# Differential attention and latent attention: row tiles turned by transposing transfers in place of TensorE transposes

## The chip, the cores and the metric

One core of a Trainium2 chip runs the kernel. The metric is the device time of one launch in microseconds (us). The kernel before takes 2170.72 us, the median of three runs (2170.44 to 2171.89).

## The reference

A decoder trunk of two layers over 256 tokens of 2048 values, all in 32-bit floats. Layer 0 has differential attention (8 heads, each with two query and two key parts of 128, of which the first 32 values are rotated by position), layer 1 multi-head latent attention (16 heads; each query has 128 plain and 64 rotated values). Behind each stands cross-attention into 256 memory tokens and a squared-ReLU MLP, and each of these adds its result to the residual stream. Cut to what the change touches:

```python
q = partial_rope(q.reshape(B, S, 2 * DA_HEADS, DA_HEAD_DIM), cos, sin, DA_ROT)
k = partial_rope(k.reshape(B, S, 2 * DA_HEADS, DA_HEAD_DIM), cos, sin, DA_ROT)
...
s = jnp.einsum('bqhcd,bkhcd->bhcqk', qi, k).astype(jnp.float32) * scale
p = jax.nn.softmax(s, axis=-1)
a = (p[:, :, 0] - lam * p[:, :, 1]).astype(v.dtype)
o = jnp.einsum('bhqk,bkhd->bqhd', a, v)
o = rms_norm(o, subln) * (1.0 - lambda_init)
return o.reshape(B, S, D_MODEL) @ wo
...
q = (c_q @ wuq).reshape(B, S, MLA_HEADS, MLA_NOPE + MLA_ROPE)
q = jnp.concatenate([q[..., :MLA_NOPE], apply_rope(q[..., MLA_NOPE:], cos, sin)], axis=-1)
```

## The kernel before

**Matrix products.** Every 32-bit product is made of three passes on TensorE, high by high, high by low, low by high. A job is 1 MB of weights: `load` (L189) fetches it on SP's queue into one of seven `raw` buffers, ScalarE casts each half to its high part (`whi`, L221) and VectorE subtracts for the low part (`wlo`, L222), four buffers each. A half serves 12 matmuls 512 wide for each of two row tiles of 128 tokens.

**Layer 0** goes through its heads in four groups, 0 to 3 (`attention`). For each group `project_diff` makes a chunk of 512 queries, of keys and of values; `heads_T` takes a finished row tile out of the accumulator with its scale (ScalarE), rotates it (`rope`, six operations on POOL), and turns it, so that heads stand on the partitions; then it is split into high and low parts (`split`, L366 on ScalarE and L367 on VectorE). Scores, softmax and weighted values of a group (`attend_diff`) run as side tasks between the chunks of the next. `normed` norms the weighted values of a row tile and turns them for the output product. The output weights are multiplied in pairs, by seven products of sums in place of eight; for some of the sums a second load is added onto a `raw` buffer by an accumulating load that POOL issues (L1003). In group 3 those pair products (`pr`) alternate with the projections (here: the weave).

**Turning a tile** goes in two ways. On TensorE: four transposes of 128x128 (`flip`, L174, called by `transpose4`) into a bank of the accumulator, or into a further one (`side_bank`, with `spare`). By transfers: ScalarE copies the tile as two planes of 16-bit words (`half_words`, L377), POOL issues a 256 KB store of them to a buffer in DRAM (`turned`, L379), SP issues a transposing transfer back (`turned_by_dma`, L384, tile `landed`). The second way is taken for group 1's queries and keys, group 2's queries, the weighted values of groups 0 and 1, and parts of the MLP.

**Layer 1** holds the rotated queries of two groups at a time in one buffer (`rotary_queries`, L1708 to L1733): two pieces of four heads each; a piece is rotated on POOL, written with its high part (L1721, ScalarE) and its low part (L1722, VectorE) side by side, and turned on TensorE through a side bank.

**What sets the order.** TensorE executes in the order in which the program issues. Side tasks are generators: one yields the time that its next step needs at least (`T_ROT` 12, `T_SHORT` 11, `T_LAND` 7, `T_TURN` 2.6 us by the program's own clock), and `pump` takes whichever is due between matmuls. The order on ScalarE, VectorE and POOL is set by a scheduler when the kernel is built; loads on SP, transposing transfers and accumulating loads stay in program order. Each engine executes its own list in order, and a wait at its head holds what is behind.

Of the kernel before, what the change touches and what calls it, by code (L numbers as in the profile page):

```python
# [18 lines left out]
P = 128  # L19
D = 2048  # L20
S = 256
NT = 2
# [30 lines left out]
def trunk(ctx, tc, x, xT, xT0, mem, memT, positions, gcols, gfinal, lam_vecs, consts, W, out):  # L53
    nc = tc.nc
# [77 lines left out]
    class Held:  # L132


        def __init__(self, tile=None):
            self.held = tile
            self.tasks = []
            self.part = None

        @property  # L140
# [21 lines left out]
    def give_back():  # L162
        free_banks[0] += 1
# [403 lines left out]

    def heads_T(ps, t, scale, dst, rot=None, spare=False, given=None, by_dma=False):


        def task():
            while given and not given():
                yield 0.5
            e = evacuate(ps, scale() if given else scale)
            if rot:
                cos, sin, heads, half = rot
                rope(e.rearrange("p (h d) -> p h d", h=heads), cos, sin, heads, half)
            if by_dma:
                yield T_ROT - 3.0 if rot else 0.2
                there = half_words(e)  # L580
                yield T_SHORT
                landed = turned_by_dma(there)
                yield T_LAND
                split(dst, t, landed)
                yield T_TURN
                return
            yield T_ROT + (14.0 if given else 0.0) if rot else T_EV
            b = ps
            if spare:
                b = yield from side_bank()  # L590
            split(dst, t, transpose4(e, b))
            if spare:
                give_back()
            yield T_TURN

        dst.run(task())
# [152 lines left out]
    def attend_diff(q, k, v, dst, coef, subcols, slack=0.0):  # L749
# [34 lines left out]
        def normed(t, blocks, out):  # L784
# [11 lines left out]
            )  # L796
            if dst.part:
                yield T_NORM
                give_back()
                there = half_words(os)  # L800
                yield T_SHORT
                landed = turned_by_dma(there)
                yield T_LAND
                split(dst, t, scaled(landed, subcols, dst.part(t)))
                yield T_TURN
                return
# [415 lines left out]
    ahead = raw_tile()  # L1222
# [173 lines left out]
    def attention(project, attend, mid, gcol, pairs=()):  # L1396
# [6 lines left out]
        for gi in range(4):  # L1403
            o = Held()
            if pairs and gi < 2:
                o.part = lambda t, gi=gi: pairs["A"].part(t, gi)
                first.append(o)
            attend(held, o)
            if pairs and gi == 2:
# [165 lines left out]
    def project_diff(gi):  # L1575
        q, k = Held(), Held()
        for i, dst in enumerate((q, k)):
            ps = matmul_chunk(acts, by_k=gi == i == 0)
            for t in range(NT):
                heads_T(  # L1580
                    ps[t], t, (lambda i=i, t=t: da_scales[i][t]) if gi == 0 else da_scales[i][t], dst, (cos[:, t, :hd], sin[:, t, :hd], 4, hd),
                    spare=gi == 3, given=(lambda: da_scales) if gi == 0 else None, by_dma=gi == 1 or (gi, i) == (2, 0),
                )
# [119 lines left out]
    def rotary_queries(gi):  # L1703
# [5 lines left out]

        def rotated(i, qr, ahead):  # L1710

            for task in ahead:
                yield task
            for t in range(NT):
                rope(rows[t][:, i], cos[:, t, hd:], sin[:, t, hd:], 4, hm)
            yield T_ROT
            es = []
            for t in range(NT):
# [3 lines left out]
                nc.vector.tensor_tensor(e[:, :, 64:], o, e[:, :, 0:64], ALU.subtract)  # L1722
                es.append(e)
            yield T_EV
            for t in range(NT):
# [8 lines left out]
        for i in range(2):  # L1734
            qr = Held(both[:, 4 * i : 4 * i + 4])
            qr.run(rotated(i, qr, ahead))
            ahead = qr.tasks
            rotary[gi + i] = qr
# [168 lines left out]
```

## Time and profile before

| | |
|---|---|
| time, median of 3 runs | 2170.72 us |
| the profiled execution's span | 2169.0 us |
| TensorE busy | 2155.4 us (99%) |
| VectorE busy | 1740.2 us (80%) |
| ScalarE busy | 1465.6 us (68%) |
| POOL busy | 221.0 us (10%) |
| moved by DMA | 543.89 MB, mean 251 GB/s |
| transposing transfers | 66 |

PE is TensorE's matmuls, PEld its weight loads, DVE VectorE, ACT ScalarE, POOL GpSimd, SP SyncE; SPq is SP's DMA queue. In a row of the timeline stand the start and the length in us, engine, line, operation, output and inputs by the program's names, the shape and a count; in brackets the idle time ahead of it and what ended that.

### The profile page before, as it was taken

Reading aid. Unit: us, or ns where it says so; the run is one execution under the profiler, and the core shown is the slowest. Engines: PE = TensorE matmul, PEld = TensorE weight load, DVE = VectorE, ACT = ScalarE, POOL = GpSimd, SP = SyncE. Lnnn points to the kernel's source line nnn. Section 1 sums busy time; section 2 is a strip of 40 time slices with the busy share of each in tenths; the row PEclk is TensorE's granted clock in tenths of the full one; section 3 lists DMA queues with packets and bytes.
Section 4 is the critical chain, followed back from the end, with each engine's and each line's share of the span. In section 5 each row is a group of like instructions: output and inputs, shape, how many; then the busy total and the mean of one; then the engine's idle time right before and its main releaser. Section 6 shows DMA issues by size and latency. Waiting matters only on the chain.

```text
span 2169.0 us, 27519 instructions
## 1 busy us (share of the span) xinstructions
PE 2155.4 (99%) x10187; PEld 1805.5 (83%) x10187; DVE 1740.2 (80%) x1962; ACT 1465.6 (68%) x1938; POOL 221.0 (10%) x336
## 2 busy tenths in 40 slices
PE   9999999999999999999999999999999999999998
PEld 7888888888888888888889988888888888888887
DVE  6656878788788889788886878778888888888887
ACT  7556756666767777776665755666777778677665
POOL 1113210001000000000000420000000000000001
PEclk9999999999999999999999999999999999999999
DMA  9477896548989999998986344645998999999895
GB/s 386 151 248 234 260 293 222 194 151 267 297 280 267 308 282 256 319 274 260 306 251 218 103 170 155 221 168 182 283 299 292 258 317 280 266 285 310 254 315 149
DMA packets 151863, 543.89 MB, mean 251 GB/s; under 512 B 79536, under 2 KB 79920, under 8 KB 92848
## 3 DMA queue, kind: packets, MB, share of 16 engines
q1 hardware_dynamic: 134496, 440.14, 56.9%
q0 software_dynamic: 16800, 101.20, 22.5%
q8 instruction: 80, 1.31, 0.2%
q10 hardware_dynamic: 432, 0.79, 0.1%
q14 instruction: 55, 0.45, 0.1%
HBM read 505.38 MB, written 19.40 MB: 242 GB/s over the span
## 4 chain that ended last, share of the span: by engine, by line
PE 95%; DVE 3%; DMA 1%; issue 1%; ACT 0%; DVEq 0%; POOLq 0%; POOL 0%
PE mm L170 62%; PE pr L170 28%; PE ax L170 3%; DVE wlo L222 1%; DMA raw<-in_mlp_wup_dram 1%; PE ax L174 1%; PE mm L174 1%; DVE raw L887 0%; DVE unit L391 0%; ACT whi L221 0%; DVE x L545 0%; DMA raw<-in_da_wqkv_dram 0%; PE pr L174 0%; DVE p L680 0%; DVE ev L1722 0%
## 5 line engine op out<-in xcount | busy, mean ns | idle before, releaser
L222 DVE TENSOR_TENSOR wlo<-raw,whi 128x1024 fp32r<-128x1024 f32 (+3 forms) x946 | 1138.8, 1217 | 335.5 <-ACT whi L221 313.7
L221 ACT CAST whi<-raw 128x1024 fp32r<-128x1024 f32 (+2 forms) x945 | 985.3, 1045 | 576.8 <-PE mm L170 420.0
L170 PE MATMUL mm<-whi,unit 128*128 128x512 f32 (+2 forms) x4000 | 1271.2, 389 | 1.3 <-DVE unit L391 0.9
L170 PEld LDWEIGHTS mm<-whi,unit 128*128 128x128 f32 x4000 | 749.1, 188 | 149.6 <-DVE unit L391 1.7
L170 PE MATMUL mm<-wlo,unit 128*128 128x512 f32 (+2 forms) x2000 | 774.1, 387 | 0.2
L170 PE MATMUL pr<-whi,unit 128*128 128x512 f32 x1912 | 610.5, 389 | 0.0
L170 PEld LDWEIGHTS mm<-wlo,unit 128*128 128x128 f32 x2000 | 376.2, 188 | 72.8 <-DVE wlo L222 3.0
L170 PEld LDWEIGHTS pr<-whi,unit 128*128 128x128 f32 x1912 | 358.8, 188 | 73.4
L170 PE MATMUL pr<-wlo,unit 128*128 128x512 f32 x956 | 372.3, 389 | 1.5 <-DVE wlo L222 1.5
L170 PEld LDWEIGHTS pr<-wlo,unit 128*128 128x128 f32 x956 | 179.7, 188 | 40.0 <-DVE wlo L222 3.6
L379 POOL DMA_DIRECT2D turned<-planes x66 | 37.7, 572 | 673.5 <-ACT planes L377 661.2
L887 DVE TENSOR_TENSOR raw<-raw,raw 128x2048 f32<-128x2048 f32 x40 | 91.5, 2288 | 8.8 <-DMA raw<-in_mlp_wup_dram 8.6
L545 DVE TENSOR_TENSOR x<-x,mm 128x512 f32<-128x512 f32 x128 | 85.3, 682 | 14.1 <-PE mm L170 14.0
L879 POOL DMA_DIRECT2D raw<-in_mlp_wup_dram x48 | 43.4, 905 | 447.8 <-DVE wlo L222 445.2
L431 POOL TENSOR_TENSOR rs<-rs,mhalf 128x1 f32<-128x1 f32 (+1 forms) x26 | 24.9, 962 | 408.1 <-DVE rs L430 408.0
L222 DVE TENSOR_TENSOR wlo<-unit,whi 128x1024 fp32r<-128x1024 f32 x48 | 57.3, 1221 | 5.2 <-ACT whi L221 4.0
L221 ACT CAST whi<-unit 128x1024 fp32r<-128x1024 f32 x48 | 49.8, 1053 | 9.7 <-PE pr L170 9.7
L377 ACT COPY planes<-p 128x1024 uint16<-128x1024 uint16 x48 | 50.0, 1041 | 0.3
L170 PE MATMUL mm<-unit,whi 128*128 128x256 f32 x256 | 46.9, 285 | 0.0
L425 ACT ACTIVATE junk<-x 128x512 bf16<-128x512 f32 (+1 forms) x57 | 35.3, 620 | 10.1 <-DVE x L1092 5.0
L1457 ACT ACTIVATE p<-p,r 128x512 f32<-128x512 f32 x42 | 30.4, 724 | 16.4 <-DVE p L962 7.4
L170 PEld LDWEIGHTS mm<-unit,whi 128*128 128x128 f32 x256 | 40.2, 192 | 0.3
(199 smaller groups left out, 1280.7 us busy)
## 6 DMA issues: line engine op xcount, KB each, us to landing
raw<-in_mlp_wdown_dram SPq DMA_DIRECT2D x128, 1024.0 KB, 7.3
raw<-in_mlp_wup_dram SPq DMA_DIRECT2D x120, 1024.0 KB, 6.9
raw<-in_mlp_wup_dram POOLq DMA_DIRECT2D x48, 1024.0 KB, 9.1
raw<-in_da_wqkv_dram SPq DMA_DIRECT2D x45, 1024.0 KB, 9.8
turned<-planes POOLq DMA_DIRECT2D x66, 256.0 KB, 6.4
raw<-in_da_wo_dram SPq DMA_DIRECT2D x16, 1024.0 KB, 7.0
raw<-in_ca_wkv_dram SPq DMA_DIRECT2D x16, 1024.0 KB, 6.7
raw<-in_mlp_wdown_dram POOLq DMA_DIRECT2D x16, 1024.0 KB, 10.7
```

Of the source, the lines that this page charges most:

```text
L170: return nc.tensor.matmul(o, stationary, moving, start=start, stop=stop, skip_group_check=onto)
L174: nc.tensor.transpose(o, src, ident)
L221: nc.scalar.copy(hi, r)
L222: nc.vector.tensor_tensor(lo, r, f32(hi), ALU.subtract)
L377: nc.scalar.copy(planes, src.bitcast(U16).rearrange("p (w s) -> p s w", s=2))
L379: nc.gpsimd.dma_start(there.rearrange("(q s) w -> q s w", s=2), planes)
L425: return nc.scalar.activation(junk[:, : src.shape[1]], src, AF.Square, scale=scale, accum_out=acc)
L431: nc.gpsimd.tensor_tensor(r[:, :n], r[:, :n], mhalf.broadcast_to([P, n]), ALU.pow)
L545: nc.vector.tensor_tensor(xc, xc, ps, ALU.add)
L879: tc.keep_in_program_order(nc.gpsimd.dma_start(onto, src, accum_op=ALU.add))
L887: nc.vector.tensor_tensor(o, o, q, ALU.add)
L1457: nc.scalar.activation(r, src, AF.Relu, scale=rstd[t])
```

## The change

Eighteen row tiles leave the first way for the second: the queries and keys of groups 0 and 3 and the keys of group 2 (ten tiles), the weighted values of group 2 (two, by the new mark `sent`), and in layer 1 three of the four held pieces of rotated queries (six tiles; the first piece stays on TensorE). TensorE has 72 transposes fewer; ScalarE has 18 copies to planes, POOL 18 stores and SP 18 transposing transfers more. For group 0 the step ahead of the turn waits `T_ROT + 14`. In `rotary_queries` the rotation is a task of its own, and a piece's rotation waits for that of the piece before, no longer for its transposes. The branch with a spare bank goes.

```diff
-    def heads_T(ps, t, scale, dst, rot=None, spare=False, given=None, by_dma=False):
+    def heads_T(ps, t, scale, dst, rot=None, given=None, by_dma=False):
...
             if by_dma:
-                yield T_ROT - 3.0 if rot else 0.2
+                yield T_ROT + (14.0 if given else -3.0) if rot else 0.2
                 there = half_words(e)
                 yield T_SHORT
                 landed = turned_by_dma(there)
@@
-            yield T_ROT + (14.0 if given else 0.0) if rot else T_EV
-            b = ps
-            if spare:
-                b = yield from side_bank()
-            split(dst, t, transpose4(e, b))
-            if spare:
-                give_back()
+            yield T_EV
+            split(dst, t, transpose4(e, ps))
@@
-            if dst.part:
+            if dst.part or dst.sent:
...
-                split(dst, t, scaled(landed, subcols, dst.part(t)))
+                split(dst, t, scaled(landed, subcols, dst.part and dst.part(t)))
@@
+            o.sent = bool(pairs) and gi == 2
@@
-                    spare=gi == 3, given=(lambda: da_scales) if gi == 0 else None, by_dma=gi == 1 or (gi, i) == (2, 0),
+                    given=(lambda: da_scales) if gi == 0 else None, by_dma=True,
@@
-        def rotated(i, qr, ahead):
-
+        def turned_rows(i, ahead):
             for task in ahead:
                 yield task
             for t in range(NT):
                 rope(rows[t][:, i], cos[:, t, hd:], sin[:, t, hd:], 4, hm)
             yield T_ROT
+
+        def rotated(i, qr, roped):
+
+            yield roped
...
+            if gi + i:
+                sent = [half_words(e.rearrange("p h d -> p (h d)")) for e in es]
+                yield T_SHORT + T_EV
+                es = [turned_by_dma(there) for there in sent]
+                yield T_LAND
+                for t in range(NT):
+                    nc.scalar.copy(qr[:, :, t * P : (t + 1) * P], es[t])
+                yield T_TURN
+                return
@@
             qr = Held(both[:, 4 * i : 4 * i + 4])
-            qr.run(rotated(i, qr, ahead))
-            ahead = qr.tasks
+            ahead = [Task(turned_rows(i, ahead))]
+            qr.run(rotated(i, qr, ahead[0]))
```

The order moves at three places. VectorE, start of the weave, before. `wlo` are splits of weights, `rs_2112` is the row norm on which POOL's first accumulating load (into `raw_1940`) waits:

```order
212 L1092 TENSOR_TENSOR x_84<-x_84,pr_2212 128x512
213 L437 TENSOR_REDUCE tot_2110<-ss_2093 128x1
214 L760 TENSOR_TENSOR rsum_2160<-rsum_2160,coef 128x4
215 L222 TENSOR_TENSOR wlo_2030<-raw_2027,whi_2029 128x1024
216 L430 TENSOR_SCALAR rs_2112<-tot_2110 128x1
217 L766 TENSOR_SCALAR a_2163<-p_2154,rsum_2160 128x128 x2
218 L654 TENSOR_TENSOR ax_2250<-ax_2250,mask 128x2x128
219 L222 TENSOR_TENSOR wlo_2034<-raw_2027,whi_2033 128x1024
220 L767 SCALAR_TENSOR_TENSOR a_2163<-p_2154,rsum_2160,a_2163 128x128
221 L624 RECIPROCAL rsum_2203<-ssum_2198 128x2
222 L767 SCALAR_TENSOR_TENSOR a_2163<-p_2154,rsum_2160,a_2163 128x128
```

And now; the norm is `rs_2119`, the accumulated buffer `raw_1948`:

```order
207 L223 TENSOR_TENSOR wlo_2033<-raw_2030,whi_2032 128x1024
208 L223 TENSOR_TENSOR wlo_2037<-raw_2030,whi_2036 128x1024
209 L1347 COPY memr_2098<-rs_2095 128x1
210 L650 TENSOR_TENSOR ax_2221<-ax_2221,mask 128x512
211 L223 TENSOR_TENSOR wlo_2132<-raw_2129,whi_2131 128x1024
212 L611 TENSOR_REDUCE nmax_2235<-ax_2221 128x4
213 L438 TENSOR_REDUCE tot_2117<-ss_2100 128x1
214 L431 TENSOR_SCALAR rs_2119<-tot_2117 128x1
215 L223 TENSOR_TENSOR wlo_2136<-raw_2129,whi_2135 128x1024
216 L1347 COPY memr_2122<-rs_2119 128x1
```

The norm stood behind the first half of an output product's weights (`raw_2027`). It now stands behind both halves of those (`raw_2030`) and the first half of the projection's weights after them (`raw_2129`).

POOL, in the weave, before: group 3's queries are rotated (`ev_2511`), then come accumulating loads; nothing is stored:

```order
110 L564 TENSOR_TENSOR rope_2516<-ev_2511,sin 128x4x16
111 L565 TENSOR_TENSOR ev_2511<-rope_2513,rope_2514 128x4x16
112 L566 TENSOR_TENSOR ev_2511<-rope_2515,rope_2516 128x4x16
113 L1003 DMA raw_1940<-in_da_wo_dram 128x2048
114 L1003 DMA raw_2417<-in_da_wo_dram 128x2048 x2
115 L561 TENSOR_TENSOR rope_2824<-ev_2822,cos 128x4x16
```

POOL at the same place now. `turned_2542` and `turned_2643` are group 2's weighted values, `turned_2590` and `turned_2594` group 3's queries:

```order
114 L380 DMA turned_2542<-planes_2540 128x1024
115 L564 TENSOR_TENSOR rope_2490<-ev_2486,cos 128x4x16
116 L565 TENSOR_TENSOR rope_2491<-ev_2486,sin 128x4x16
117 L566 TENSOR_TENSOR ev_2486<-rope_2488,rope_2489 128x4x16
118 L567 TENSOR_TENSOR ev_2486<-rope_2490,rope_2491 128x4x16
119 L999 DMA raw_1948<-in_da_wo_dram 128x2048
120 L999 DMA raw_2395<-in_da_wo_dram 128x2048
121 L432 TENSOR_TENSOR rs_2561<-rs_2561,mhalf 128x2
122 L380 DMA turned_2590<-planes_2588 128x1024
123 L380 DMA turned_2594<-planes_2592 128x1024
124 L380 DMA turned_2643<-planes_2641 128x1024
125 L999 DMA raw_2395<-in_da_wo_dram 128x2048
```

The stores of group 3's queries stand behind two accumulating loads.

SP, the same stretch, before: weight loads alone:

```order
86 L189 DMA raw_2567<-in_da_wo_dram 128x2048
87 L189 DMA raw_2591<-in_da_wqkv_dram 128x2048
88 L189 DMA raw_2661<-in_da_wqkv_dram 128x2048
89 L189 DMA raw_2707<-in_da_wqkv_dram 128x2048
90 L189 DMA raw_2742<-in_da_wo_dram 128x2048
91 L189 DMA raw_2766<-in_da_wqkv_dram 128x2048
```

SP now:

```order
93 L190 DMA raw_2598<-in_da_wqkv_dram 128x2048
94 L385 DMA_TRANSPOSE landed_2651<-turned_2542 128x4x256
95 L190 DMA raw_2659<-in_da_wqkv_dram 128x2048
96 L385 DMA_TRANSPOSE landed_2698<-turned_2590 128x4x256
97 L385 DMA_TRANSPOSE landed_2700<-turned_2594 128x4x256
98 L190 DMA raw_2709<-in_da_wqkv_dram 128x2048
99 L385 DMA_TRANSPOSE landed_2742<-turned_2643 128x4x256
100 L190 DMA raw_2751<-in_da_wo_dram 128x2048
101 L190 DMA raw_2780<-in_da_wqkv_dram 128x2048
102 L190 DMA raw_2867<-in_da_wqkv_dram 128x2048
```

Four transposing transfers stand between the loads; a load behind one of them is issued after it.

More of the change, by code (lines that the diff above doesn't have):

```diff
@@ L138, in __init__ @@
             self.part = None
+            self.sent = False
         @property
```

## The prediction

> **What bounds the kernel now.** I read the page first, the head for the span, the busy times and the shares of the chain that ended last.
>
> ```profile
> span 2169.0 us, 27519 instructions
> PE 2155.4 (99%) x10187; PEld 1805.5 (83%) x10187; DVE 1740.2 (80%) x1962; ACT 1465.6 (68%) x1938; POOL 221.0 (10%) x336
> PE 95%; DVE 3%; DMA 1%; issue 1%; ACT 0%; DVEq 0%; POOLq 0%; POOL 0%
> ```
>
> TensorE is the bound nearly everywhere: 95% of the chain. What it does not execute is time won one for one, as long as its inputs come as early as before; the question is what they come through then. The span is 1.7 us under the median of the runs (2170.7). I make the sum as a difference to the span and put the same difference to the median. About 0.2%, 4.3 us, is what a measurement of this kernel can tell from no change, so the median has to come under 2166.4 to count as faster and over 2175.1 to count as slower.
>
> Next the costs of the two routes: TensorE's own rows around one batch of eight transposes, then each step of the route by transfer (ns min/median/max, and us to landing).
>
> ```profile
> 62.00 0.39 PE L170 MATMUL mm<-whi,unit 128*128 128x512 f32 x1
> 62.23 1.03 PE L174 MATMUL mm<-identr,ev 128*128 128x128 f32 x8
> 63.02 0.48 PE L170 MATMUL mm<-whi,unit 128*128 128x512 f32 x1
> 63.34 0.40 PE L170 MATMUL mm<-wlo,unit 128*128 128x512 f32 x1
> 63.57 0.62 PE L170 MATMUL mm<-whi,unit 128*128 128x512 f32 x2
> ...
> L377 ACT COPY planes<-ev x14: 1032/1042/1053, 103.3 to 1531.2; 128x1024 uint16<-128x1024 uint16 x14
> ...
> L379 POOL DMA_DIRECT2D turned<-planes x66: 539/572/760, 104.7 to 1995.0; - x66
> ...
> DMA to landing us min/median/max: 2.3/6.4/9.0
> ...
> L384 SPq DMA_TRANSPOSE landed<-turned x66: 1227/1634/9474, 115.1 to 2014.3; - x66
> ...
> DMA to landing us min/median/max: 3.1/6.0/14.0
> ```
>
> Matmuls overlap, so the price of one is the distance of starts, not its length. A 512-wide one costs 63.57 - 63.34 = 0.23 us. From 62.23 to 63.34 lie eight transposes and one such matmul: 1.11 - 0.23 = 0.88, so 0.11 us a transpose.
>
> Third, how busy the stages are into which the new transfers fall. Columns: sum, PE, PEld, DVE, ACT, POOL, granted clock, share of the 16 DMA engines, GB/s.
>
> ```profile
> 60.00:80.00 20.00, 20.00 (x98) 16.74 (x97) 11.91 (x13) 10.56 (x13) 0.00 (x0) 1.00 0.40 149
> 80.00:100.00 20.00, 20.00 (x104) 16.89 (x102) 14.38 (x28) 12.35 (x27) 1.73 (x6) 1.00 0.16 52
> 220.00:230.00 10.00, 10.00 (x51) 8.45 (x50) 9.87 (x23) 9.74 (x28) 2.41 (x2) 1.00 0.60 240
> 240.00:320.00 80.00, 80.00 (x377) 66.87 (x376) 62.07 (x67) 49.11 (x60) 20.47 (x33) 1.00 0.98 302
> 1180.00:1300.00 120.00, 119.27 (x785) 109.37 (x784) 95.12 (x151) 76.24 (x139) 36.29 (x64) 1.00 0.43 152
> ```
>
> Group 0 (60 to 100 us) and the latent layer (1180 to 1300) have DMA engines to spare. The weave, in which group 3's projections alternate with the products of the output weights, does not: at its start VectorE and ScalarE are full (9.87 and 9.74 of 10 us), and then the DMA engines are, 0.98 over 80 us.
>
> **The change part by part.** *Transposes off TensorE.* 18 tiles of four: 72 x 0.11 = **-7.9 us**. All lie on the bound engine, none under anything else.
>
> *The held rotary pieces.* TensorE waited for their subtraction on VectorE (L1722) in the latent layer:
>
> ```profile
> 1234.09 0.28 PE L170 MATMUL mm<-unit,wlo 128*128 128x256 f32 x1
> 1234.42 0.63 PE L174 MATMUL ax<-identr,ev 128*128 128x128 f32 x4
> 1235.27 0.66 PE L174 MATMUL ax<-identr,ev 128*128 128x128 f32 x4 [0.22 <-DVE ev L1722]
> ...
> 1250.87 0.28 PE L170 MATMUL ax<-raw,unit 128*128 128x256 f32 x1
> ...
> 1266.18 0.38 PE L174 MATMUL ax<-identr,p 128*128 128x128 f32 x2
> 1267.02 1.09 PE L174 MATMUL ax<-identr,ev 128*128 128x128 f32 x8 [0.46 <-DVE ev L1722]
> ```
>
> A 256-wide matmul takes half of 0.23, so the first batch came 1234.42 - 1234.09 - 0.12 = 0.21 late; the second 0.85 - 4 x 0.11 = 0.41; the third 0.84 - 2 x 0.11 = 0.62. Together **-1.2 us**, for those transposes are gone. What is late next: the pieces themselves. Their first reader is the score matmul at 1250.87. In the new order L1722 stands one weight split earlier on VectorE, so by the transfers they are split at about 1232: planes 1.0 each, store 2.3 to 6.4, transposing transfer 3.1 to 6.0: landed between 1240 and 1246, in a stage whose DMA share is 0.43. Scores come some 1.5 us sooner than in this trace; 2 to 8 us are left, cost 0. The same goes for the two pieces of the next group, which have longer. Without that cover it would be up to 4 us.
>
> *Group 0's queries and keys.* Their scores move behind the value chunk and most of the next group's query chunk, about 20 us later, in a stage with a DMA share of 0.40 and 0.16. Planes, store, transfer and copy take 1 + 6.4 + 6 + 0.6 = 14 us by the medians: cost 0, at most 5 if all take their longest (9.0 and 14.0).
>
> *ScalarE and VectorE.* 18 planes copies at 1.04 are 19 us of ScalarE, spread over 68% busy; VectorE has as many instructions as before. Cost 0 except where ScalarE is full, below.
>
> *The weave's start.* The first load that accumulates into the weight buffer waits on POOL behind a row norm; the norm waits on VectorE. Rows of POOL, ScalarE and TensorE, then the landing times of these loads:
>
> ```profile
> 229.68 0.56 POOL L431 TENSOR_TENSOR rs<-rs,mhalf 128x1 f32<-128x1 f32 x1 [4.07 <-DVE rs L430]
> 230.44 0.95 POOL L1003 DMA_DIRECT2D raw<-in_da_wo_dram  x1 [0.20 <-issue]
> ...
> 238.62 2.95 ACT L221 CAST whi<-raw 128x1024 fp32r<-128x1024 f32 x3 [3.08 <-DMA raw<-in_da_wo_dram]
> ...
> 242.47 0.39 PE L170 MATMUL pr<-whi,unit 128*128 128x512 f32 x1
> ...
> DMA to landing us min/median/max: 8.1/10.4/18.8
> ...
> L222 DVE TENSOR_TENSOR wlo<-raw,whi 128x1024 fp32r<-128x1024 f32 (+3 forms) x946 | 1138.8, 1217 | 335.5 <-ACT whi L221 313.7
> ```
>
> ScalarE stood 3.08 us for that load, TensorE did not: its product began at 242.47, with the first half cast at 239.7 (three casts in 2.95) and split 1.2 later, a margin of 1.6 to 2.8 us. In the new order the product comes 242.47 - 24 x 0.11 (the transposes gone by then) - 1.2 (other work put behind it) = 238.6, and the norm stands behind a split of the next projection's weights (two splits later than before). That split's buffer comes free when TensorE ends the first half of an earlier job. From there to the product TensorE has, counted in the new order, three halves of that projection (12 matmuls, 2.72 us each), two halves of a pair product (1.36 each) and three groups of scores (1.2, 0.7, 0.7): 13.5 us. The chain takes cast and split 1.0 + 1.2, norm and POOL 1 + 0.8, load 8.1, cast 1.0, and 0 to 1.5 of queueing on VectorE: 13.1 to 14.6, and 1.2 more until the low half is there. TensorE waits 0 to 2.5; I take **+2.0**, from the upper part, because VectorE's row is full there. Ends 0 and 5 (a landing at the median 10.4 in place of 8.1).
>
> *Group 3's queries.* Their two stores are issued on POOL behind two more accumulating loads, and land after them; the transfers stand on SP ahead of weight loads; ScalarE's two copies of the landed tiles stand ahead of the cast of the weights that TensorE needs at about 287 (238.6, the 2 us above, and 46 us of work between: 16 pieces of 2.72 and 3 us of scores and values). The row for a pair of such loads, and what SP has waited for stores so far:
>
> ```profile
> 261.75 1.81 POOL L1003 DMA_DIRECT2D raw<-in_da_wo_dram  x2
> ...
> SPq L384 <- DMA turned<-planes: 88.9, 12, 14.1
> ...
> DMA packets 151863, 543.89 MB, mean 251 GB/s; under 512 B 79536, under 2 KB 79920, under 8 KB 92848
> ...
> L366 ACT CAST unit<-landed x10: 607/616/621, 121.8 to 1415.5; 128x512 fp32r<-128x512 f32 x10
> ```
>
> Issued at about 259, the pair lands after 10.4 to 18.8, at 270 to 278; the stores 2 to 3 later; the transfers 3.1 to 6.0, the second 1.2 behind: 276 to 288; two copies and the cast, 0.62 x 2 + 1.05: 279 to 290. So 0 to 3, and with a transfer at its longest, 14.0, 11. The weave also takes six turns more, each 0.25 MB stored and read again over the same engines, 0.5 MB at 251 GB/s, 2 us: 12 us more of DMA time in a stage at 0.98. I take **+2.5**, ends 0 and 11. Keys of group 3 and the weighted values have 5 us more room: in these ends.
>
> Sum: -7.9 - 1.2 + 2.0 + 2.5 = **-4.6 us**: span 2164.4, median **2166.1**. It is just inside "faster".
>
> A rule speaks against the change. The Trainium skill, VectorE: DVE Perf Modes, "The three transpose paths", puts a 128x128 transpose at 390 ns on TensorE and 1309 ns by DMA, and its rules advise TensorE where PSUM will do. If that counted as time on the path, 72 of them would lose 66 us (an estimate from that page); the rows above, 0.11 us on the bound engine against a route that no row of the chain's shares shows, do not bear it out.
>
> **The rivals.** *All of it hidden.* The weave's waits fall into the margins. For it: before, TensorE's rows are full from 240 to 320 although the engines around it were full too. Against: the margin at 242.47 shrinks by 4 us. -9.1: span 2159.9, median 2161.6.
>
> *The weave is bound by transfers.* Each load behind a turn lands later by part of the 12 us, and loads that accumulate have little room. For it: 0.98. Against: the loads are issued ahead, as buffers come free, so part of the delay is swallowed. Stalls of 9 instead of 4.5: -0.1, median about 2170.6, no change.
>
> *Slower: SP and ScalarE held in order.* Place: group 3's queries. The store lands behind two accumulating loads at 278, the transfer waits on SP with the next weight loads behind it and takes 14.0 in a full stage, and ScalarE's copies keep the casts behind them: 278 + 3 + 14 + 2.3 = 297 against 287, 10 to 11 us, then the held loads, each landing 10 us after issue, 4 more. With 2 at the start: 16 to 17, so +7 to +8, median about 2178. It decides from stalls of 13.4 us in all. For it: SP has waited up to 14.1 us for one store. Against: such waits have not put SP into the chain's shares.
>
> **How the numbers follow.** The forecast (stalls of 2 to 7 us, 2163.5 to 2168.5) gets 0.42, all hidden 0.18, bound by transfers (2168.5 to 2175) 0.25, slower 0.15. The forecast lies on both sides of 2166.4, 0.30 under it and 0.12 over. Faster: 0.18 + 0.30 = 0.48. Same: 0.12 + 0.22 = 0.34, the transfers' case giving 0.03 to the other side. Slower: 0.15 + 0.03 = 0.18. Range: the hidden case at the low end, 2161; at the high end the transfers' case whole, 2175; the slower case, and what of the hidden one comes out under 2161, are left out.
>
> **What would show it.** TensorE: 72 transposes fewer, no row that waits for L1722. At the weave's start, a wait of TensorE at the first product of the accumulated weights, released by ScalarE or VectorE, behind a ScalarE wait for that load. In the weave, ScalarE waiting for landed tiles, SP for stores. Wrong would be: no wait of TensorE there (then 2161.6), or over 7 us in the weave, or a wait at group 0's or the latent scores, which I hold at nothing.

## The result and the profile after

| | before | after |
|---|---|---|
| time, median | 2171.3 us (2170.4 to 2172.9) | 2205.1 us (2191.1 to 2209.9) |
| ratio | | 1.0144 (95% interval 1.0128 to 1.0161) |
| span of the profiled execution | 2169.0 us | 2208.1 us |

The change makes the kernel 34 us slower, outside the range and on the other side of the forecast. The profiled execution, 2209.9 us, is the slowest of the four after, and the pieces below are its own. The page after, head, busy times and shares of the chain:

```profile
span 2208.1 us, 27503 instructions
PE 2165.6 (98%) x10115; PEld 1805.6 (82%) x10115; DVE 1738.7 (79%) x1962; ACT 1480.1 (67%) x1956; POOL 227.3 (10%) x354
PE 78%; DMA 5%; DVE 3%; issue 2%; POOL 1%; ACT 1%; DVEq 0%; POOLq 0%
```

TensorE has 72 instructions fewer and is busy 10.2 us longer. The 72 are worth 7.9 us, so its other work ran 18 us slower. The rest of the 39.1 us is idle time: 2208.1 - 2165.6 against 2169.0 - 2155.4, 28.9 us more. Which stage? The same pieces of the chain, before and then after (start us, length, what):

```profile
372.07 15.02 PE mm L170 x66
...
1148.82 32.80 PE mm L170 x192
...
1426.78 21.81 PE mm L170 x96
```

```profile
410.56 15.00 PE mm L171 x66
...
1190.21 32.80 PE mm L171 x192
...
1464.67 21.81 PE mm L171 x96
```

Up to the first piece, which lies behind layer 0's attention, 38.5 us are lost: that is the whole loss. From there to the latent queries (the second piece) it is 2.9 more (776.75 to 779.65), over the latent stage, up to the third piece, 3.5 less (277.96 to 274.46), and to the end 1.2 more. Now the stretches that the prediction showed, in the same columns:

```profile
60.00:80.00 20.00, 20.00 (x90) 16.59 (x89) 12.01 (x12) 11.25 (x14) 1.10 (x2) 1.00 0.74 233
80.00:100.00 20.00, 20.00 (x89) 16.55 (x89) 10.36 (x10) 9.93 (x12) 4.03 (x12) 1.00 0.63 217
240.00:320.00 80.00, 60.45 (x232) 47.75 (x233) 41.75 (x50) 38.62 (x54) 13.84 (x22) 0.83 0.88 172
1180.00:1300.00 120.00, 120.00 (x770) 113.57 (x769) 89.23 (x144) 75.78 (x136) 36.49 (x64) 1.00 0.49 169
```

Group 0 and the latent stage are full, as forecast; the 0.73 us that TensorE missed in the latent row before are gone. The weave lost: TensorE is busy 60.45 of 80 us at a granted clock of 0.83, and the DMA engines move 172 GB/s at a share of 0.88, where they moved 302 at 0.98. By the share they are nearly as occupied, and they carry little more than half. The chain through that stretch:

```profile
231.89 11.11 DMA raw<-in_da_wo_dram
243.03 1.05 ACT whi L222
...
270.09 35.63 DMA raw<-in_da_wo_dram
305.76 15.15 issue
...
327.59 8.70 DMA turned<-planes
336.30 15.77 DMA landed<-turned
```

Three places: the weave's first accumulating load, 11.11 us; the second of a pair, 35.63 us, where the second of that pair took 18.8 before; and a store and a transposing transfer of group 3's keys, 8.70 and 15.77 us, behind which TensorE waits 5.6 us for the cast. TensorE at the first (idle time in brackets):

```profile
239.18 0.39 PE L171 MATMUL mm<-wlo,unit 128*128 128x512 f32 x1
239.41 0.39 PE L171 MATMUL mm<-whi,unit 128*128 128x512 f32 x1
244.12 0.49 PE L171 MATMUL pr<-whi,unit 128*128 128x512 f32 x1 [4.33 <-ACT whi L222]
245.39 0.80 PE L171 MATMUL pr<-wlo,unit 128*128 128x512 f32 x1 [0.77 <-DVE wlo L223]
...
246.83 0.63 PE L171 MATMUL pr<-wlo,unit 128*128 128x512 f32 x1
247.26 1.06 PE L171 MATMUL pr<-whi,unit 128*128 128x512 f32 x2
```

It waits 4.33 and 0.77 us, and then starts matmuls 0.43 us apart (246.83 to 247.26) in place of 0.23 (239.18 to 239.41), until about 251. So this wait costs its length and some 3 us of slow matmuls. The Trainium skill, TensorE: Matmul & The Clock Gate, "Part 1: The HAM clock gate", says that after an idle window of about 3.4 us the array runs at half its clock until it has been busy that long; the trace agrees with the half, 0.43 against 0.23, but the slow matmuls here last longer, from 244.12 to about 251.

SP and POOL at the second place, and then the landing times of the transposing transfer at 269.12, of the two accumulating loads, and of the weight load that SP issued behind that transfer (L190), each from the view of its line between 260 and 290, or 270 and 280:

```profile
267.48 0.33 SPq L190 DMA_DIRECT2D raw<-in_da_wqkv_dram  x1
269.12 1.23 SPq L385 DMA_TRANSPOSE landed<-turned  x1
270.45 0.52 SPq L190 DMA_DIRECT2D raw<-in_da_wqkv_dram  x1
306.47 2.58 SPq L385 DMA_TRANSPOSE landed<-turned  x2
```

```profile
269.48 1.79 POOL L999 DMA_DIRECT2D raw<-in_da_wo_dram  x2
...
271.73 1.40 POOL L380 DMA_DIRECT2D turned<-planes  x2
```

```profile
DMA to landing us min/median/max: 25.0/25.0/25.0
...
DMA to landing us min/median/max: 30.4/33.0/35.6
...
DMA to landing us min/median/max: 32.2/32.2/32.2
```

The transfer at 269.12 is the first row tile of group 2's weighted values, 256 KB. It takes 25.0 us. Beside it are a load that SP issued 1.6 us ahead, two accumulating loads (30.4 and 35.6 us) and SP's next load (32.2 us). The two stores of group 3's queries, issued from 271.73 on, land behind them at 306.4 and 307.0, so SP, which waits for those, issues nothing from 271 to 306.47. Who waits, on VectorE, ScalarE and TensorE:

```profile
294.18 0.69 DVE L373 TENSOR_TENSOR xg<-landed,gsub 128x512 f32<-128x512 f32 x1 [10.92 <-DMA landed<-turned]
```

```profile
299.99 1.99 ACT L222 CAST whi<-raw 128x1024 fp32r<-128x1024 f32 x2 [17.83 <-DMA raw<-in_da_wo_dram]
```

```profile
296.06 0.79 PE L171 MATMUL mm<-wlo,unit 128*128 128x512 f32 x1 [9.32 <-DVE wlo L223]
```

VectorE stands 10.92 us at the head of its list for the landed values, with a split of weights behind it, and TensorE stands for that split. Then ScalarE has stood 17.83 us for the first load of the pair, with all casts behind it.

### The profile page after: what moved, and what is told of

It is laid out like the page before. It is cut to its first block, busy times and chain, and to the rows that moved or that the text cites. A ratio compares the mean times of both kernels' runs of the same rounds, so it can differ in the third digit from the quotient of the medians.

```text
span 2208.1 us, 27503 instructions
## 1 busy us (share of the span) xinstructions
PE 2165.6 (98%) x10115; PEld 1805.6 (82%) x10115; DVE 1738.7 (79%) x1962; ACT 1480.1 (67%) x1956; POOL 227.3 (10%) x354
## 4 chain that ended last, share of the span: by engine, by line
PE 78%; DMA 5%; DVE 3%; issue 2%; POOL 1%; ACT 1%; DVEq 0%; POOLq 0%
PE mm L171 49%; PE pr L171 26%; DMA raw<-in_mlp_wup_dram 2%; DMA raw<-in_da_wo_dram 2%; PE ax L171 2%; DVE wlo L223 1%; PE ax L175 1%; PE mm L175 1%; DMA landed<-turned 1%; DVE raw L883 1%; ACT whi L222 0%; DMA turned<-planes 0%; DVE unit L392 0%; DVE x L546 0%; POOL rope L563 0%
## 5 line engine op out<-in xcount | busy, mean ns | idle before, releaser
L380 POOL DMA_DIRECT2D turned<-planes x84 | 48.0, 574 | 718.3 <-ACT planes L378 693.6
L883 DVE TENSOR_TENSOR raw<-raw,raw 128x2048 f32<-128x2048 f32 x40 | 91.5, 2288 | 11.0 <-DMA raw<-in_mlp_wup_dram 10.7
L1454 ACT ACTIVATE p<-p,r 128x512 f32<-128x512 f32 x42 | 30.4, 723 | 16.5 <-DVE p L958 7.4
```

The lines of the kernel that those rows point to most:

```text
L380: nc.gpsimd.dma_start(there.rearrange("(q s) w -> q s w", s=2), planes)
L883: nc.vector.tensor_tensor(o, o, q, ALU.add)
L1454: nc.scalar.activation(r, src, AF.Relu, scale=rstd[t])
```

## The experiments

The loss "up to x66" is that piece's start less 372.07, from each kernel's own chain: it measures layer 0 apart from the rest, which varies by some 3 us between executions. It is of one execution of each kernel. The theory: transfers collide in the weave. The main rival: plain order, in which SP and ScalarE wait for late stores.

**Transfers alone.** The kernel leaves out the trunk and runs each case between two barriers.

The cases in short (transfer: a transposing one of 256 KB; acc: an accumulating 1 MB load of POOL):

```text
(1) transfer   (2) acc   (3) acc acc   (4) SP load x2   (5) acc acc + transfer
(6) load load of POOL + transfer   (7) SP load, transfer, SP load
(8) acc acc + SP load x2   (9) acc + transfer x2   (10) load load of POOL
```

> This kernel computes nothing of the trunk: it runs the disputed transfers by themselves, one group after the other, each group started when the one before has landed. Collision theory (a transposing transfer and accumulating loads in flight together slow each other far beyond their sum): a transposing transfer alone 3 to 4 us, one accumulating load alone 5 to 8, two about 10 to 13; the transposing transfer beside two accumulating loads 15 us or more, and these two 20 or more; beside plain loads on SP's queue it lands in under 8. Rivals (bandwidth, or waits of the queues in order): beside two accumulating loads it lands within the sum of the times alone, under 16 for all, and beside plain loads on either queue it is the same.

The transposing transfer alone, and with two accumulating loads:

```profile
L89 SPq DMA_TRANSPOSE landed<-turned x1: 1317/1317/1317, 13.9 to 13.9; - x1
...
DMA to landing us min/median/max: 3.2/3.2/3.2
...
L101 SPq DMA_TRANSPOSE landed<-turned x1: 1240/1240/1240, 50.3 to 50.3; - x1
...
DMA to landing us min/median/max: 6.5/6.5/6.5
```

The expected collision did not come: 6.5 us, and the two loads took 8.3 and 12.6 as against 7.7 and 12.1 without it. A transfer and accumulating loads alone are not the cause, or not in this arrangement. Beside two plain loads of POOL (case 6) the transfer took longer, 11.7 us, and landed 0.4 us behind the second.

**Parts of the change undone.** Group 2's weighted values back on TensorE:

```diff
-            o.sent = bool(pairs) and gi == 2
+            o.sent = False
```

> Group 2's weighted values go back to TensorE (8 transposes), all other turns as changed. Collision theory: the transposing transfer that took 25 us beside two accumulating loads is gone, and with it some 22 to 26 us; the later collision of group 3's keys stays, if its transfers still meet a load: about 2182. Queue theory (SP and ScalarE held in order behind group 3's queries, whose stores stand behind two accumulating loads): little changes, about 2200. Bandwidth theory: a third of the weave's loss back, about 2192.

2182.8 us, ratio 1.0059 (1.0043 to 1.0076); up to x66 387.02 - 372.07 = 15.0 lost in place of 38.5. This is the number of the collision (about 2182), not of the order (about 2200). Without the transfer at 269 the pair of loads takes 13.4 and 18.1 us. What is left is in part the order: the stores of group 3's queries land at 286.6 and 287.2 behind the pair, SP issues nothing from 269 to 286.6, and from 289.3 on five loads within 2.4 us.

Group 3's queries and keys back (through a further bank, as before):

```diff
-                    ..., by_dma=True,
+                    spare=gi == 3, ..., by_dma=gi < 3,
```

> Group 3's queries and keys go back to TensorE through a side bank (16 transposes), group 2's values stay with the transfers. Collision theory: the later collision is gone, about 12 us, the earlier one stays: about 2194. Queue theory: what held SP and ScalarE is gone, about 2172. Bandwidth theory: two thirds of the loss back, about 2180.

2187.2 us, 2175.2 to 2191.0 over five runs, ratio 1.0067 (1.0044 to 1.009); no theory gave that number (2194, 2172 or 2180). The profiled run is the one of 2175.2; its transfer of the values took 7.3 us and the pair 12.0 and 18.8, so in it the collision was absent, although SP's load was issued 1.6 us ahead of the transfer and the pair 0.4 us behind it, as in the changed kernel. The order is the same in each run, but not what happens; that the other four have the collision is likely and not shown, for none of them was profiled.

Both back:

> Both of these go back to TensorE (24 transposes): of the change stay groups 0 and 2's queries and keys and the latent pieces, 48 transposes off TensorE. All theories: the weave's loss is gone; left are -5.3 for the transposes, -1.2 for the waits on the held pieces, and 2 to 5 for the weave's start: 2167 to 2169.

2175.7 us, ratio 1.0023 (1.0013 to 1.0034): up to x66 5.8 lost. Expected was a gain. Of the changes at the weave and just ahead of it only group 2's keys are left. The next kernel puts them back too; group 0 and the latent layer stay changed.

```diff
-                    ..., by_dma=True,
+                    spare=gi == 3, ..., by_dma=gi < 2 or (gi, i) == (2, 0),
```

> Of the change stay group 0's queries and keys and the latent pieces, 40 transposes off TensorE; group 2's keys too go back. If the weave's start was made late by group 2's keys (their transfers hold SP ahead of the loads for the row norm), its 8 us of waits and slow clock are gone: -4.4 for the transposes, -0.9 to -1.2 for the waits on the held pieces: 2165 to 2166. If the start is late for other reasons (the scores moved in groups 0 to 2), it stays at 2172 to 2175.

2168.5 us (expected 2165 to 2166), ratio 0.9991 (0.9982 to 0.9999), up to x66 1.7 gained. The stretch of the weave's start, with both back, and with group 2's keys back as well:

```profile
230.00:250.00 20.00, 15.03 (x60) 11.74 (x59) 11.55 (x27) 9.01 (x23) 2.39 (x3) 0.84 0.69 187
```

```profile
230.00:250.00 20.00, 20.00 (x103) 16.96 (x102) 16.38 (x26) 11.30 (x22) 2.52 (x3) 1.00 0.71 181
```

So the keys' eight transposes cost 377.89 - 370.35 = 7.5 us net, 8.4 with the 0.9 that they save. In the changed kernel their transfers stand on SP at 204.80 and 208.82, ahead of the loads of the memory rows that the norm needs; the first accumulating load is issued 1.45 us later than before (231.89 against 230.44) and lands in 11.1 instead of 8.1. Between the two kernels of this pair that load lands in 11.1 and 11.0, and what differs is its issue: at 231.03 with the keys on transfers, behind a norm at 230.12; at 224.60 without, behind a norm at 223.63. Of the memory rows ScalarE squares the first as it lands, at 213.12 against 208.30; the last had landed at 221.18 against 213.68 and is squared among casts at 227.52 against 218.09. So the norm is late in part by its rows, and in part by the places of its steps in the lists of ScalarE and VectorE; the parts were not separated.

**The condition of the collision.** Five groups of four rounds, since in the trunk SP's load was ahead of the transfer and in the first study it was not:

```text
(1) transfer, acc acc
(2) SP load, transfer, acc acc
(3) transfer, SP load, acc acc
(4) transfer, acc acc, store store
(5) SP load, transfer, SP load, acc acc, store store
```

> Transfers by themselves again, nothing of the trunk: five groups, each four times over, of one transposing transfer with two accumulating loads from POOL: alone; behind a plain load on SP; ahead of a plain load on SP; with two stores queued behind the loads; and with all of these, as the changed kernel has them in its weave at 269 us, where the transfer took 25 us and the loads 30 and 36. The first transfer experiment had 6.6 us for the transfer and 8.3 and 12.6 for the loads. If meeting is enough by chance, some of the 20 transfers take 15 us or more, in every group. If it takes the neighbours, only the last groups have such. If none has, the stall comes of something else in the kernel at that place, such as waits that hold the queues in order.

The transfers of groups 2, 3, 4 and 5:

```profile
L97 SPq DMA_TRANSPOSE landed<-turned x4: 1226/1227/1261, 73.0 to 131.1; - x4
...
DMA to landing us min/median/max: 16.3/18.9/28.4
...
DMA to landing us min/median/max: 6.8/6.9/6.9
...
DMA to landing us min/median/max: 6.8/6.9/7.0
...
DMA to landing us min/median/max: 17.8/20.2/24.3
```

With an SP load ahead of it, and only then, the transfer takes 16 to 28 us, in eight rounds of eight, and lands behind the pair. Issued ahead of that load it takes 6.8 to 6.9 (with none, in group 1, once 13.1). But the pair itself is drawn out in four of the eight only: its second load takes 15.3, 15.6, 20.4 and 28.2 us in group 2, and 31.2, 22.2, 16.4 and 15.3 in group 5, where it takes 15.4 in group 3 with the same three loads. So the collision of the trunk, in which the loads are drawn out too, comes with an SP load ahead and does not come each time; the run with group 3's turns undone had not shown it either. (In groups 2 and 5 the transfer also starts 0.1 to 0.2 us behind the first accumulating load and not ahead of it. In the trunk it started 0.36 us ahead and was drawn out all the same.)

The values' transfers 14 us later, behind those of group 3's queries:

```diff
-                yield T_SHORT
+                yield T_SHORT if dst.part else T_SHORT + 14.0
```

> The changed kernel, with one number changed: group 2's weighted values wait 14 us longer between their store and their transposing transfer, so that the transfer stands behind those of group 3's queries on SP and cannot meet the two accumulating loads. Collision theory: the first stall goes, 20 to 25 us: about 2183. Queue theory: SP is held behind the same stores as before, so 2198 or more.

2182.3 us, ratio 1.0054 (1.0039 to 1.007); the pair of loads takes 13.0 and 16.9 us, and no transfer more than 15.6. All 18 tiles still go by transfers, and 23 us come back: the place is the cause, not the number. SP is still held behind the stores of group 3's queries, from 268.5 to 287.1, and by that rival it would have been 2198 or more: the rival alone does not make the loss.

The loads of POOL overwrite instead of adding, in the same order (the sums of weights are left out):

```diff
-                nc.gpsimd.dma_start(..., accum_op=ALU.add)
+                nc.gpsimd.dma_start(...)
```

> The changed kernel, but POOL's second loads in the weave overwrite their buffer instead of adding onto it (the sums of weights are left out, the transfers and their order stay). If it is the adding that collides with transposing transfers, the stall at 269 to 306 us goes: about 2180. If any load of POOL's queue does it, the stall stays: 2195 to 2205.

2177.4 us, 2174.9 to 2187.1, ratio 1.004 (1.0023 to 1.0057). The median is near what was expected if the adding collides (about 2180). The profiled run, of 2187.1, still has a transfer of 20.5 us beside plain loads of POOL of 21.9 and 25.1. So the adding isn't needed for a collision; whether it makes one more frequent or longer is not shown.

What of group 2 of the second study matters:

```text
(1) SP load, transfer             (2) SP load, transfer, load load of POOL
(3) SP load, transfer, acc        (4) SP load, transfer once that has landed, acc acc
(5) SP load, plain 256 KB load of SP, acc acc
```

> Transfers alone once more, nothing of the trunk is computed: it leaves all of it out. Six groups of four rounds, each round between two barriers. (1) a 1 MB load on SP, the 256 KB transposing transfer behind it, nothing on POOL; (2) the same beside two plain loads of POOL; (3) beside one accumulating load of POOL; (4) beside two accumulating loads, but the transfer waits until SP's load has landed; (5) as in (4) without that wait and with a plain 256 KB load in place of the transposing one. (The groups are told apart by their order.) Theory (a transposing transfer that follows an SP load still in flight, beside loads of POOL, is drawn out): (1) 5 to 7 us, (2) and (3) 12 us or more, (4) under 9, (5) under 12. First rival (it is only the share of the engines that a transfer behind 3 MB of loads gets, transposing or not): (5) as long as the 16 to 28 us of the study before, (4) over 12. Second rival (it takes an accumulating load): (2) under 9.

There are these five groups. The transfers of groups 1 to 4:

```profile
L94 SPq DMA_TRANSPOSE landed<-turned x4: 1233/1288/1437, 14.5 to 34.4; - x4
...
DMA to landing us min/median/max: 5.1/5.4/5.5
...
L98 SPq DMA_TRANSPOSE landed<-turned x4: 1551/1671/1712, 41.2 to 77.4; - x4
...
DMA to landing us min/median/max: 10.4/10.7/11.1
...
DMA to landing us min/median/max: 11.5/15.3/19.4
...
DMA to landing us min/median/max: 10.9/11.0/11.1
```

Without loads of POOL nothing happens (5.4). Beside two plain loads the transfer takes 10.4 to 11.1, where 12 or more was expected: it lands 0.7 to 0.8 us behind the second and draws nothing out. Beside one accumulating load it takes 11.5 to 19.4 and draws that load out with it, to between 11.2 and 19.1, where it took 7.7 alone. Group 4 missed its number (11 instead of under 9): behind a landed load the transfer still lands just behind the pair. But the pair then takes 10.7 and 15.2 in all four rounds, never 28. Plain in place of transposing (group 5) it is 8.8, and lands ahead of both. So there are two effects. A transposing transfer that starts among loads of POOL lands just behind the last of them. And with a load of SP in flight ahead of it, accumulating loads beside it can be drawn out: beside two of them that happened in four rounds of eight, where in the twenty rounds that lacked that load of SP, or the transposing, the second of the two took 18.1 us at most.

**The transfer held back in the trunk.** The changed kernel, but SP copies four bytes a row out of the weight load ahead before each transfer of the values, and so waits for it:

```diff
...
+        if late:
+            cell = landed.bitcast(F32).rearrange("p k t -> p (k t)")[:, 0:1]
+            tc.keep_in_program_order(nc.sync.dma_start(cell, last[0][:, 0:1]))
         tc.keep_in_program_order(nc.sync.dma_start_transpose(landed, there))
...
-                landed = turned_by_dma(there)
+                landed = turned_by_dma(there, dst.sent)
```

> The kernel after, with one thing added: ahead of each of the two transposing transfers of group 2's weighted values SP copies four bytes a row from the last weight buffer that it loaded to the buffer into which the transfer will write; so the transfer starts only when that load has landed, and the loads behind it wait too. The order is otherwise the changed kernel's, the same 18 tiles go by transfers. Theory (drawn out is what meets in flight: a load of SP's queue, the transfer behind it and two accumulating loads; where the transfer waited for the load, alone on the chip, the accumulating loads took 10.7 and 15.3 us and the transfer 11): the two loads at 269 land at about 280 and 285 in place of 300 and 306, some 15 to 20 us come back: 2185 to 2192, ratio 1.007 to 1.010. Rival (the transfer behind the loads is enough, wherever SP's load is): the loads land at 295 or later, 2200 to 2208, ratio over 1.013.

2181.7 us, ratio 1.0051 (1.0036 to 1.0066). The same pair of loads, and the chain at that place:

```profile
L1006 POOL DMA_DIRECT2D raw<-in_da_wo_dram x2: 883/1035/1187, 267.2 to 267.9; - x2
...
DMA to landing us min/median/max: 9.1/11.2/13.4
```

```profile
271.45 9.89 DMA landed<-raw
281.35 1.24 SPq L392
```

9.1 and 13.4 us in place of 30.4 and 35.6; the loss up to x66 falls from 38.5 to 13.5. Two small copies take 25 us out of layer 0, rather more than expected. The copy itself took 9.9 us beside the pair, to 281.3; the pair had landed by then, and the transfer behind it took 3.2. So this kernel, like the one with the values 14 us later, keeps the transfer away from the pair altogether. It shows that the meeting is the cause; that SP's load in flight is part of the condition rests on the studies of transfers alone.

The same with group 2's keys back on TensorE:

```diff
-                    ..., by_dma=True,
+                    spare=gi == 3, ..., by_dma=(gi, i) != (2, 1),
```

> The kernel with the waiting transfers, and in addition group 2's keys turned on TensorE as before, so that nothing new stands on SP ahead of the rows that the norm at the weave's start waits for. It separates the two losses once more: the weave's start was a loss of 7 to 8 us by the kernels with and without these keys. Theory: 7 to 8 us less than the kernel with the waits alone, less 0.9 us of transposes that come back: 2178 to 2185, ratio 1.004 to 1.007, and TensorE full from 230 to 250 us. Rival (the start's loss is only moved to the next load that is late): within 3 us of that kernel.

2183.2 us, ratio 1.0059 (1.0043 to 1.0076): not faster. TensorE is nearly full from 230 to 250 (19.48 of 20), but then

```profile
PE mm L171 <- DVE wlo L227: 12.4, 1, 12.4
```

```profile
276.23 0.69 DVE L377 TENSOR_TENSOR xg<-landed,gsub 128x512 f32<-128x512 f32 x1 [12.25 <-DMA landed<-turned]
```

VectorE stood for the landed values again, because the copy ahead of their transfer took 10.0 us. The rival's number came out, by the experiment's own wait. The start's wait is gone here too: the first accumulating load is issued at 225.16, against 231.41 with the keys on transfers. What that is worth, the two kernels with both parts back and with the weave as before tell.

**The latent layer alone.** Before, with the latent layer's part:

```diff
...
+            if gi + i:
+                sent = [half_words(e.rearrange("p h d -> p (h d)")) for e in es]
+                ...
```

> The kernel before with the latent layer's part alone: three of the four held pieces of rotated queries turned by transfers, 24 transposes fewer; layer 0 is the kernel before's. By the stage's own measure in all kernels that have this part (277.96 us before, 274.46 to 274.49 with it) the time falls by 3.5 us: 2167.4, ratio 0.9984. Rival (the part's gain is taken back behind it by the transfers, as the kernel with group 0's part and this one, -2.2 where 40 transposes fewer promised -5.6, leaves possible): -1 to -2, 2169.5. If it gains 3.5, what that kernel lacked was lost in layer 0's part or in the products between, not here.

2169.3 us, ratio 0.9993 (0.9984 to 1.0002). The stage takes 1421.64 - 1147.18 = 274.46 us, the 3.5 less once more, and the profiled span is 2165.3, 3.7 under before's. The median of eleven runs gains 1.2 only, which is the rival's number (2169.5), and its interval reaches over 1. The eleven lie between 2166.7 and 2172.2, and waits for the MLP's weight loads come and go on the chain (5.96 us at 1553.91 here, 12.69 at 972.17 in the profile before). What decides those was not tried.

## Why the prediction was wrong

**Right.** *Transposes off TensorE and the held pieces*: 24 x 0.11 and 1.2 make 3.8 for the latent stage, measured 3.5 in every kernel with that part. *Group 0's cost of 0*: its 16 transposes are 1.8 by the sum, and the kernel with the weave as before gains 1.7 up to x66.

**The weave's start, +2.0, ends 0 and 5.** The mechanism was as told: norm later, load later, TensorE waiting on the cast; only the memory rows on SP and their squares on ScalarE, which the keys' transfers put back, were not in it. It cost 8.4. The wait itself was 5.1 (4.33 + 0.77), just past the upper end: the load took 11.1, close to the median of 10.4 that the end of 5 used. The rest, some 3 us, is the slow clock behind a wait, which the sum left out at every wait. It was not to be seen in the profile before, where the clock stood at 1.00 in all the stretches shown.

**Group 3's queries, +2.5, ends 0 and 11.** This step failed. Two things lay in it. Group 3's turns alone, with the values back, cost 15.0 - 5.8 = 9.1 us net, 10.9 with the 1.8 that their 16 transposes save: at the upper end, far from the value taken. The queueing in order (stores behind the pair of loads, SP held) is the slower rival's mechanism and part of it; whether it is all of it is not shown. The other thing, 25 us in the profiled execution, was in no term: the transposing transfer of the *weighted values*, for which "5 us more room" was all that the prediction had, draws out the pair of accumulating loads, and what stands behind them waits. The prediction priced loads, stores and transfers each by the rows of their own line, as if a transfer in flight could only be late itself. It took 14.0, the longest transfer before, for a tail. It was the sign: in the trace before, the transfers of the MLP that shared 2.5 us or more with an accumulating load took 9.1 to 14.0 us (587.68 to 600.49, 663.85 to 677.52, 1759.73 to 1773.72), all others 3.1 to 9.9. The former had two to four loads of SP in flight ahead of them as well, so that trace does not tell which of the two it is. Nor did the prediction name VectorE's instruction on the landed values, which stood at the head of its list.

**The estimate of 12 us of DMA time** for six more turns held engines to be shared by bytes. The share of 0.88 at 172 GB/s shows what that misses: the share adds up the times of the packets, and here they took longer for the same bytes.

**The rivals.** "Bound by transfers" gave stalls of 9 us, "slower" 16 to 17; the stalls (waits, and slow matmuls behind them) came to 38.5 + 5.3 (48 transposes) = 43.8 us up to x66. The parts, each from its own pair of kernels, are 8.4 at the start, 25.0 from the collision and 10.9 from group 3's turns: 44.3. That they add up is no proof by itself, for the steps from the changed kernel over the values, then group 3's turns, then the keys to the weave as before would add up in any case (24.4, 10.9 and 8.4); it says that holding the values' transfer back is worth what putting the values back is. The 25.0 hold more than the wait at 296: in the kernel with the values back the piece of group 3's keys is 8.68 us and not 15.77, and TensorE's wait behind it 3.3 and not 5.6. The bound named for being wrong, over 7 us in the weave, was passed five times over. The rule of the Trainium skill that the prediction cites is not borne out as a rule of time per transpose: where the cover holds, 40 transposes fewer did not slow the kernel (2168.5 against 2170.4 us).

**What stays open.** Why the three kinds of transfer draw each other out. In the trace's packet records packets of 256 bytes, 1024 between 270 and 294 us, are the transfer's: 830 start by 276 us, 57 in the next 4 and the last shortly before 294; single 8 KB packets of the pair took 12.65 and 15.19 us there, against a median of 0.63 between 266 and 310. That tells where the time lies, not why. Open too is what decides, with an SP load ahead, whether it happens. The Trainium skill, Advanced Engine Details and Errata, "X-Bar Transpose (TRN2)", calls transposing DMAs as fast as regular ones; for the small one here that does not hold among loads of POOL (8.8 plain, 11.0 transposing, and up to 28.4); apart it took 3.2 us, and no run has a plain one apart.

## What to carry to other kernels

Before moving work to transfers in a full stage, look in the trace for each transfer that starts while loads of another queue are in flight, and take its time there, and that of the loads beside it, rather than the median of its line: the longest value of a line is often a state that the change will visit more. Price a wait of TensorE of a few microseconds with some 3 us of slow matmuls on top. Where a transposing transfer has to share a stage with accumulating loads, issue it when they have landed, or ahead of SP's load (6.8 to 6.9 us, though only with the transfers alone on the chip). And look in the new order, on SP, ScalarE and VectorE, for what stands ahead of the steps that a later stage's first load waits for.

## What the runs showed that was not expected

- A 256 KB transposing transfer: 3.2 us alone, 5.4 behind an SP load, 6.5 to 7.0 ahead of two accumulating loads (once 13.1), 11 among them, 16 to 28 between an SP load in flight and them, in half of these rounds with the second of those loads drawn out from 15 to as much as 31.
- A copy of four bytes a row took 9.9 and 10.0 us among two accumulating loads, 1.7 and 2.1 without.
- DMA share and throughput parted: 0.88 at 172 GB/s after, 0.98 at 302 before, in the same stretch.
- The same order gives different times: 2175.2 to 2191.0 us with group 3's turns undone, 2191.1 to 2209.9 with the whole change.
